# Layer 0's 16 by 16 inverses: masked copies moved to ScalarE on both sides of a transfer, and one load of all diagonal blocks

## The chip, the cores and the metric

The kernel runs on one core of a Trainium2 chip. The metric is device time in microseconds (us) of one execution; times of several runs are given by their median. The engines are TensorE (PE in the profile; its weight loads are PEld), VectorE (DVE), ScalarE (ACT), GpSimd (POOL) and SyncE (SP), which here only issues transfers (DMAs). Each engine works through an instruction queue of its own, whose order is fixed when the kernel is built.

## The reference, cut to what matters

A two-layer trunk over 1024 time steps and 1024 channels. Layer 0 has two groups of heads, each followed chunk by chunk (here 128 steps to a chunk): RWKV-7 (`wkv7_scan`) and gated DeltaNet. In chunked form both need, for each chunk and head, the inverse of a unit triangular 128 by 128 matrix:

```
    amat = jnp.where(strict, jnp.einsum('bhncd,bhnsd->bhncs', kb, k) * decay, 0.0)
    rhs = jnp.concatenate([v * beta[..., None], kb * jnp.exp(gc)[..., None]], -1)
    sol = lax.linalg.triangular_solve(amat, rhs, left_side=True, lower=True, unit_diagonal=True)
```

Then come the output projection, a squared-ReLU MLP and a gated embedding, and in layer 1 chunked attention with the same MLP; all of these are large matrix products.

## The kernel before, in words

Layer 0 works through 16 units: for each half of the time steps (512 each) and each of four head pairs, one RWKV unit and one DeltaNet unit in turn. A unit passes the stages `in` (projections), `front`, `mid`, `back` and `post`; several units are under way at once, as generators that a small planner (`Trunk.run`) takes forward by a virtual clock, with waiting times from the table `LAT`. The planner sets the order in which the code is written down. From that, the scheduler of the tile framework makes the order of each engine's queue at build time, with a cost model of its own: an instruction goes in where the model thinks that its inputs are ready. On the chip that order is kept.

Each unit has one inversion, so there are 16. The odd ones (1, 3, ... 15) are RWKV's with eight 128 by 128 matrices (tile `N`, four chunks of two heads), the even ones DeltaNet's with four (tile `Ng`). `inverse_start`, called in `front`, does the smallest blocks, and its steps are one chain:

- L411: the matrices go to scratch memory (`scr`), a row of 512 bytes for each matrix and partition, all matrices of a partition side by side (4 KB for eight).
- L415: the 16 by 16 diagonal blocks come back as `Bq` (`subb` in the profile), one block to a partition, 8 blocks to a matrix; one load for each matrix, eight or four.
- L423 and L425: GpSimd sets the start of the inverse `X` (tile `sub`), upper triangle and ones on the diagonal, in two passes. L430 and L432: 14 steps of a product and a sum on GpSimd.
- L433 and L434: GpSimd makes two masked copies, one transposed, of the blocks that have an even number.
- L436 and L438: copy, inverse and masked copy go out to scratch memory (`z`), 768 numbers for each block, and come back as `Xp` with 16 rows of a block on 16 partitions, 48 numbers each.

`inverse_end`, called in `mid`, builds the 128 by 128 inverse from them with small matmuls into a PSUM tile `iz`; its first matmuls are `iz<-Xp,N` (or `iz<-Xp,Ng`). ScalarE copies its results (L463, L479, L488, L490, L501).

Beside it, TensorE runs the projections, `dps<-xg,whi` and `dps<-xg,wlo`: 128 by 512 products, 24 to a 128-row weight tile. Each weight tile is loaded by SP (`wraw`), and split by ScalarE (`whi`, L318) and VectorE (`wlo`, L319). In `back`, RWKV's recurrence has for each chunk a copy on ScalarE of `bk` to `bm` (L999), a copy `W<-ch` (L1036) and matmuls that need them (`pm<-AR,bm`, `ch<-W,F`). `tp<-AR,bk` and `sc<-KQ` are the matmuls that give `N` and `Ng`; `o` (L1070, L1072) and `po` belong to the ends of recurrences.

Of the kernel before, what the change touches and what calls it, by code (L numbers as in the profile page):

```python
# [8 lines left out]
F32 = mybir.dt.float32  # L9
F32R = mybir.dt.float32r  # L10
I32 = mybir.dt.int32
AF = mybir.ActivationFunctionType
ALU = mybir.AluOpType
# [4 lines left out]
P = 128  # L18
# [94 lines left out]
class Trunk:  # L113
# [140 lines left out]
    def masks(self, cst):  # L254
# [4 lines left out]
        for j, op in enumerate((ALU.is_ge, ALU.is_gt, ALU.is_ge)):  # L259
# [12 lines left out]
        nc.vector.tensor_reduce(h[:, 2:3], self.ident.rearrange("p (n two) -> p n two", two=2)[:, :, 0],  # L272
                                op=ALU.add, axis=AX.X)
        self.Z16 = cst.tile([P, 8, 32], F32, tag="Z16", name="Z16")
# [132 lines left out]
    def inverse_start(self, B, G):  # L407
        nc, fr = self.nc, self.fr
        NP = 8 * G
        scr = self.dr.tile([P, G, P], F32, tag=f"scr{G}", name="scr", bufs=2)  # L410
        nc.sync.dma_start(out=scr, in_=B)  # L411
        Bq = fr.tile([NP, 16, 16], F32, tag="subb", name="subb")
        for g in range(G):
            b = scr[0:1, 0:1, 0:1]
            nc.sync.dma_start(out=Bq[8 * g:8 * g + 8],  # L415
                              in_=bass.AP(tensor=b.tensor, offset=b.offset + g * P,
                                          ap=[[16 * G * P + 16, 8], [G * P, 16], [1, 16]]))

        XX = fr.tile([NP, 16, 3, 16], F32, tag="sub", name="sub")
        X = XX[:, :, 1, :]  # L420
        tmp = fr.tile([NP, 64], F32, tag="subt", name="subt")
        E = nc.gpsimd
        E.affine_select(out=X, in_=Bq, compare_op=ALU.is_gt, fill=1.0, base=0, pattern=[[-1, 16], [1, 16]],  # L423
                        channel_multiplier=0)
        E.affine_select(out=X, in_=X, compare_op=ALU.is_ge, fill=0.0, base=0, pattern=[[-1, 16], [1, 16]],  # L425
                        channel_multiplier=0)
        for i in range(1, 15):
            n = 15 - i
            o = tmp[:, 0:i * n].rearrange("p (i n) -> p i n", i=i)
            E.tensor_tensor(o, X[:, 0:i, i:i + 1].broadcast_to((NP, i, n)),  # L430
                            Bq[:, i:i + 1, i + 1:16].broadcast_to((NP, i, n)), op=ALU.mult)
            E.tensor_tensor(X[:, 0:i, i + 1:16], X[:, 0:i, i + 1:16], o, op=ALU.add)  # L432
        E.tensor_scalar(XX[:, :, 0, :], X.rearrange("p r c -> p c r"), self.half[0:NP, 2:3], None, op0=ALU.mult)  # L433
        E.tensor_scalar(XX[:, :, 2, :], X, self.half[0:NP, 2:3], None, op0=ALU.mult)  # L434
        z = self.dr.tile([NP, 768], F32, tag=f"z{G}", name="z", bufs=2)
        nc.sync.dma_start(out=z, in_=XX.rearrange("p r w c -> p (r w c)"))  # L436
        Xp = self.mid.tile([P, G, 64], F32, tag="Xp", name="Xp", bufs=2)
        nc.sync.dma_start(out=Xp[:, :, 0:48], in_=z.rearrange("(g b) (r c) -> (b r) g c", g=G, r=16))  # L438
        return Xp

    def inverse_end(self, Xp, B, N, F):

        nc, h2 = self.nc, self.mid
        V, A, G = nc.vector, nc.scalar, nc.gpsimd
        T1, cur, X2 = Xp[:, :, 0:16], Xp[:, :, 16:32], Xp[:, :, 32:64]
        m2 = self.half[:, 1:2]
        quad = [slice(32 * i, 32 * i + 32) for i in range(4)]
        up, lo = slice(0, 64), slice(64, 128)

        def bank(w):  # L450
            return self.psm.tile([P, N, w], F32, tag="iz", name="iz")

        def new(nm, w):
            return h2.tile([P, N, w], F32, tag=nm, name=nm)


        pz = bank(16)
        for g in range(N):
            for q in quad:
                self.mm(pz[q, g, :], B[q, g, q], T1[q, g, :], start=True, stop=True)  # L460
        TZ = self.TZ[:, 0:N]
        T2, Z = TZ[0:96, :, 0:32], TZ[:, :, 0:32]
        A.activation(self.Z16[:, 0:N, 0:16], pz, AF.Copy, scale=m2)  # L463
        yield f"inverse{N}_0"
        px = bank(16)
        for g in range(N):
            for q in quad:
                self.mm(px[q, g, :], self.Z16[q, g, :], cur[q, g, :], start=True, stop=True)
        V.scalar_tensor_tensor(X2[:, :, 16:32], cur, m2, px, op0=ALU.mult, op1=ALU.add)
        V.transpose(T2, X2[0:96])  # L470
        V.transpose(TZ[quad[1], :, 32:64], X2[quad[1]])
        yield f"inverse{N}_1"

        pz = bank(32)
        for g in range(N):
            for i in (0, 2):
                self.mm(pz[quad[i + 1], g, :], B[quad[i], g, quad[i + 1]], T2[quad[i], g, :], start=True, stop=True)
        for i, cp in ((0, A.copy), (2, V.tensor_copy)):
            cp(Z[quad[i + 1]], pz[quad[i + 1]])  # L479
        for i, cp in ((2, V.tensor_copy), (3, A.copy), (0, V.tensor_copy), (1, A.copy)):  # L480
            cp(F[quad[i], :, quad[i]], X2[quad[i]])
        yield f"inverse{N}_2"
        px = bank(32)
        for g in range(N):
            for i in (0, 2):
                self.mm(px[quad[i], g, :], Z[quad[i + 1], g, :], X2[quad[i + 1], g, :], start=True, stop=True)
            self.mm(px[quad[1], g, :], X2[quad[1], g, :], Z[quad[1], g, :], start=True, stop=True)
        A.copy(Z[quad[1]], px[quad[1]])  # L488
        for i, cp in ((2, V.tensor_copy), (0, A.copy)):
            cp(F[quad[i], :, quad[i + 1]], px[quad[i]])  # L490
        yield f"inverse{N}_4"

        part = lambda t, e: t[:, e::2, :]

        def both(ps, f):
            for g in range(N):
                f(ps[up if g % 2 == 0 else lo, g, :], g)

        def out(dst, ps):
            for e, r in ((0, up), (1, lo)):  # L500
                A.copy(part(dst, e), part(ps[r], e))  # L501
        pz = bank(64)
        both(pz, lambda o, g: self.mm(o, B[up, g, lo], TZ[up, g, :], start=True, stop=True))
        out(TZ[lo], pz)
        yield f"inverse{N}_5"
        px = bank(64)
        both(px, lambda o, g: self.mm(o, TZ[lo, g, :], F[lo, g, lo], start=True, stop=True))
        out(F[up, :, lo], px)
        yield f"inverse{N}_6"
# [1754 lines left out]
```

## Time and profile before

| what | value |
|---|---|
| median of 3 runs (lowest to highest) | 2938.03 us (2933.39 to 2940.38) |
| the profiled execution, its span | 2942.2 us, 2940.5 us |
| TensorE busy, of the span | 2866.6 us, 97% |
| VectorE, ScalarE, GpSimd busy | 72%, 50%, 14% |
| mean granted TensorE clock | 0.989 |

Times in the views count from the span's start; the profiled execution is 1.7 us longer than its span. [...] "Idle before" in a row, in square brackets, names what ended an engine's wait.

### The profile page before, as it was taken

The page shows a single profiled execution, that of the slowest core. Times are in us where ns is not written, and L with a number is a line of the kernel's source. Part 1 is how long each engine was busy: PE and PEld are TensorE (multiplying, and loading weights), DVE is VectorE, ACT ScalarE, POOL GpSimd, SP SyncE. Part 2 cuts the span into 40 slices and gives each one's busy share as a digit, 9 for nine tenths or more (in the row PEclk, how much of TensorE's full clock was granted, in tenths as well). Part 3 has the DMA queues.
Part 4 walks back from the last instruction along what each step waited for, and adds up shares of the span by engine and source line. Part 5 has one row for each costly group of instructions (what it writes and reads, how often), then busy time and mean ns, then how long its engine had stood idle before and what let it go on. Part 6 is the DMA issues. An engine that isn't in the chain of part 4 may idle for free.

```text
span 2940.5 us, 46945 instructions
## 1 busy us (share of the span) xinstructions
PE 2866.6 (97%) x17286; PEld 2413.2 (82%) x17286; DVE 2107.7 (72%) x4228; ACT 1466.9 (50%) x2904; POOL 408.8 (14%) x834
## 2 busy tenths in 40 slices
PE   8999999999999999999999999999999999999999
PEld 6777778787778888888888999999888888888877
DVE  6666744555668777788887677776858777878884
ACT  4454532344347555544444566665847555544441
POOL 5434421333120000000000111111300000000000
PEclk9999999999999999999999999999999999999999
DMA  7634434333456444754424211110465444754423
GB/s 266 211 132 157 143 105 146 96 111 110 133 204 204 150 147 155 265 179 151 151 89 143 74 45 57 56 46 28 140 228 201 151 147 154 272 172 150 154 93 116
DMA packets 209479, 421.43 MB, mean 143 GB/s; under 512 B 46832, under 2 KB 49120, under 8 KB 209248
## 3 DMA queue, kind: packets, MB, share of 16 engines
q1 hardware_dynamic: 178432, 362.31, 37.6%
q10 hardware_dynamic: 30816, 56.11, 5.0%
q8 instruction: 136, 2.23, 0.3%
q14 instruction: 95, 0.78, 0.1%
HBM read 287.47 MB, written 130.87 MB: 142 GB/s over the span
## 4 chain that ended last, share of the span: by engine, by line
PE 73%; DVE 11%; DMA 8%; ACT 3%; issue 2%; POOL 2%; SPq 0%; ACTq 0%; DVEq 0%; POOLq 0%
PE dps L180 60%; PE ch L180 2%; PE po L180 2%; PE iz L180 2%; DVE act L1338 1%; PE pt L195 1%; PE pm L180 1%; PE sn L180 1%; PE tp L180 1%; DMA pn<-pnd 1%; POOL subt L430 1%; POOL sub L432 1%; DMA late<-hd 1%; DMA hb<-late 1%; DMA Xp<-z 1%
## 5 line engine op out<-in xcount | busy, mean ns | idle before, releaser
L180 PE MATMUL dps<-r,act 128*128 128x512 f32 x3720 | 865.9, 389 | 4.1 <-DVE r L1338 1.3
L180 PEld LDWEIGHTS dps<-r,act 128*128 128x128 f32 x3720 | 697.1, 188 | 152.7 <-DVE r L1338 2.1
L180 PE MATMUL dps<-xg,whi 128*128 128x512 f32 x1184 | 395.3, 414 | 11.2 <-ACT whi L318 7.5
L180 PE MATMUL dps<-wq,act 128*128 128x384 f32 x1536 | 302.2, 340 | 2.4 <-DVE vs L1994 1.5
L180 PEld LDWEIGHTS dps<-wq,act 128*128 128x128 f32 x1536 | 263.1, 188 | 5.6 <-DVE vs L1994 2.6
L180 PEld LDWEIGHTS dps<-xg,whi 128*128 128x128 f32 x1184 | 218.0, 195 | 56.9 <-ACT whi L318 7.5
L180 PE MATMUL dps<-xg,wlo 128*128 128x512 f32 x592 | 239.2, 405 | 2.0 <-DVE wlo L319 2.0
L1337 ACT CAST act<-act 128x512 fp32r<-128x512 f32 (+2 forms) x281 | 159.0, 599 | 139.9 <-PE dps L180 62.7
L1338 DVE TENSOR_TENSOR act<-act 128x512 fp32r<-128x512 f32 (+2 forms) x281 | 177.8, 661 | 3.5 <-ACT act L1337 3.4
L180 PE MATMUL dps<-act 128*128 128x512 f32 x720 | 173.5, 389 | 0.0
L1337 ACT CAST act<-late 128x512 fp32r<-128x512 f32 x210 | 123.8, 620 | 90.4 <-PE dps L180 61.8
L180 PE MATMUL dps<-late,act 128*128 128x512 f32 x672 | 164.5, 389 | 0.0
L1338 DVE TENSOR_TENSOR act<-late,act 128x512 fp32r<-128x512 f32 x210 | 139.4, 687 | 28.1 <-ACT act L1337 27.9
L180 PEld LDWEIGHTS dps<-act 128*128 128x128 f32 x720 | 135.2, 188 | 28.1
L180 PEld LDWEIGHTS dps<-late,act 128*128 128x128 f32 x672 | 125.9, 188 | 26.0
L180 PE MATMUL dps<-xw,act 128*128 128x512 f32 x576 | 143.8, 389 | 0.4 <-ACT act L1337 0.4
L1605 DVE TENSOR_TENSOR xw<-xw,dps 128x512 f32<-128x512 f32 x192 | 130.0, 682 | 16.4 <-PE dps L180 15.9
L180 PEld LDWEIGHTS dps<-xg,wlo 128*128 128x128 f32 x592 | 114.5, 193 | 27.7 <-DVE wlo L319 3.1
L180 PEld LDWEIGHTS dps<-xw,act 128*128 128x128 f32 x576 | 108.0, 188 | 23.2 <-ACT act L1337 0.8
L2117 ACT ACTIVATE pb<-pb,mx 128x640 f32<-128x640 f32 (+4 forms) x128 | 89.2, 697 | 51.9 <-DVE mx L2111 50.8
L1863 POOL MEMSET far<- 128x256 f32 x1 | 0.3, 312 | 756.0 <-PE dps L180 756.0
L1337 ACT CAST r<-act 128x512 fp32r<-128x512 f32 x126 | 76.3, 618 | 56.3 <-PE dps L180 37.8
(522 smaller groups left out, 5377.7 us busy)
## 6 DMA issues: line engine op xcount, KB each, us to landing
hb<-late ACTq DMA_DIRECT2D x196, 256.0 KB
act<-hb SPq DMA_DIRECT2D x158, 256.0 KB
late<-in_w SPq DMA_DIRECT2D x60, 512.0 KB
act<-in_w SPq DMA_DIRECT2D x112, 256.0 KB
braw<-hb SPq DMA_DIRECT2D x80, 256.0 KB
wd<-whi SPq DMA_DIRECT2D x32, 512.0 KB
wd<-wlo SPq DMA_DIRECT2D x32, 512.0 KB
wlo<-wd SPq DMA_DIRECT2D x32, 512.0 KB
```

The costliest lines, as they stand in the source:

```text
L180: return self.begin(self.nc.tensor.matmul(out, lhsT, rhs, start=start, stop=stop, skip_group_check=again))
L195: return self.begin(self.nc.tensor.transpose(out, in_, ident))
L430: E.tensor_tensor(o, X[:, 0:i, i:i + 1].broadcast_to((NP, i, n)), Bq[:, i:i + 1, i + 1:16].broadcast_to((NP, i, n)), op=ALU.mult)
L432: E.tensor_tensor(X[:, 0:i, i + 1:16], X[:, 0:i, i + 1:16], o, op=ALU.add)
L1337: A.copy(hi, s)
L1338: V.tensor_tensor(lo, s, hi.bitcast(F32), op=ALU.subtract)
L1605: V.tensor_tensor(x[n][:, hs[hf]], x[n][:, hs[hf]], ps, op=ALU.add)
L1863: nc.gpsimd.memset(self.far, 0.0)
L2117: A.activation(S, S, AF.Exp, bias=mx[:, 1:2] if nf else mx[:, 0:1], scale=-1.0, accum_out=l)
```

## The change

The matrices go out in two transfers, one for each half of them, into scratch memory laid out with a distance of P\*P+P numbers from matrix to matrix, so that all 16 by 16 blocks lie at one constant distance and come back by one load. The start of the inverse is one masking pass and a write of ones on the diagonal. GpSimd's two masked copies are gone: the transposed one is made by ScalarE before the outward transfer (new L434), and the other by ScalarE from the returned tile (new L447, at the head of `inverse_end`), so `z` has 512 numbers for each block instead of 768, and `Xp` gets 32 in a row instead of 48. From L447 on, line numbers after the change are one higher.

```diff
     def inverse_start(self, B, G):
...
-        scr = self.dr.tile([P, G, P], F32, tag=f"scr{G}", name="scr", bufs=2)
-        nc.sync.dma_start(out=scr, in_=B)
+        pitch = P * P + P
+        scr = self.dr.tile([G, pitch], F32, tag=f"scr{G}", name="scr", bufs=2)
+        d = scr[0:1, 0:1]
+        for g in (G // 2, 0):
+            nc.sync.dma_start(out=bass.AP(tensor=d.tensor, offset=d.offset + g * pitch,
+                                          ap=[[P, P], [pitch, G // 2], [1, P]]), in_=B[:, g:g + G // 2])
         Bq = fr.tile([NP, 16, 16], F32, tag="subb", name="subb")
-        for g in range(G):
-            b = scr[0:1, 0:1, 0:1]
-            nc.sync.dma_start(out=Bq[8 * g:8 * g + 8],
-                              in_=bass.AP(tensor=b.tensor, offset=b.offset + g * P,
-                                          ap=[[16 * G * P + 16, 8], [G * P, 16], [1, 16]]))
-
-        XX = fr.tile([NP, 16, 3, 16], F32, tag="sub", name="sub")
+        nc.sync.dma_start(out=Bq, in_=bass.AP(tensor=d.tensor, offset=d.offset,
+                                              ap=[[16 * P + 16, NP], [P, 16], [1, 16]]))
+
+        XX = fr.tile([NP, 16, 2, 16], F32, tag="sub", name="sub")
...
-        E.affine_select(out=X, in_=Bq, compare_op=ALU.is_gt, fill=1.0, base=0, pattern=[[-1, 16], [1, 16]],
+        E.affine_select(out=X, in_=Bq, compare_op=ALU.is_gt, fill=0.0, base=0, pattern=[[-1, 16], [1, 16]],
                         channel_multiplier=0)
-        E.affine_select(out=X, in_=X, compare_op=ALU.is_ge, fill=0.0, base=0, pattern=[[-1, 16], [1, 16]],
-                        channel_multiplier=0)
+        E.memset(flat[:, 16:512:33], 1.0)
...
-        E.tensor_scalar(XX[:, :, 0, :], X.rearrange("p r c -> p c r"), self.half[0:NP, 2:3], None, op0=ALU.mult)
-        E.tensor_scalar(XX[:, :, 2, :], X, self.half[0:NP, 2:3], None, op0=ALU.mult)
-        z = self.dr.tile([NP, 768], F32, tag=f"z{G}", name="z", bufs=2)
-        nc.sync.dma_start(out=z, in_=XX.rearrange("p r w c -> p (r w c)"))
+        nc.scalar.activation(XX[:, :, 0, :], X.rearrange("p r c -> p c r"), AF.Copy, scale=self.half[0:NP, 2:3])
+        z = self.dr.tile([NP, 512], F32, tag=f"z{G}", name="z", bufs=2)
+        nc.sync.dma_start(out=z, in_=flat)
         Xp = self.mid.tile([P, G, 64], F32, tag="Xp", name="Xp", bufs=2)
-        nc.sync.dma_start(out=Xp[:, :, 0:48], in_=z.rearrange("(g b) (r c) -> (b r) g c", g=G, r=16))
+        nc.sync.dma_start(out=Xp[:, :, 0:32], in_=z.rearrange("(g b) (r c) -> (b r) g c", g=G, r=16))
         return Xp
...
     def inverse_end(self, Xp, B, N, F):
...
         m2 = self.half[:, 1:2]
+        A.activation(X2[:, :, 0:16], cur, AF.Copy, scale=self.half[:, 0:1])
         quad = [slice(32 * i, 32 * i + 32) for i in range(4)]
```

The planner's table and rules are untouched, but the scheduler, which sees other instructions, makes another order of the queues. On TensorE the orders agree up to shortly before the first `iz` matmul of the fourth inversion, and again from the end of layer 0 on, but for some 26 rows in layer 1. Three places follow. Numbers behind names tell tiles apart and differ between the two builds.

ScalarE's queue at the third inversion, inside the recurrence of an RWKV unit, before the change:

```order
L479 COPY TZ_239<-iz_2078 32x4x32
L1168 ACTIVATE f_2187<-KQ_1794 128x512
L1128 ACTIVATE f_2293<-raw_1475,vecs_60 128x512
L999 COPY bm_241<-bk_1372 64x256
L1036 COPY W_1954<-ch_1950 128x128
L488 COPY TZ_239<-iz_2101 32x4x32
```

The same place after it:

```order
L480 COPY TZ_239<-iz_2057 32x4x32
L1169 ACTIVATE f_2166<-KQ_1772 128x512
L1129 ACTIVATE f_2267<-raw_1462,vecs_60 128x512
L434 ACTIVATE sub_1703<-sub_1703,half_145 64x16x16
L1000 COPY bm_241<-bk_1358 64x256
L1037 COPY W_1932<-ch_1928 128x128
L489 COPY TZ_239<-iz_2080 32x4x32
```

The new masked copy of this inversion's blocks (L434) stands ahead of the copies `bm` and `W` of another unit's recurrence; nothing else moved here.

ScalarE's queue at the fourth inversion, after the change (`bh` is a cast in the front of the next RWKV unit, `whi` are weight tiles for projections):

```order
L1222 ACTIVATE U_2376<-ch_2374,cs_1146 128x128
L880 ACTIVATE f_2792<-raw_2128,d_omu_69 128x512
L1000 COPY bm_241<-bk_2392 64x256
L434 ACTIVATE sub_2227<-sub_2227,half_145 32x16x16
L967 CAST bh_2795<-f_2790 128x512
L318 CAST whi_2615<-wraw_2613 128x1024
L318 CAST whi_2707<-wraw_2705 128x1024
L447 ACTIVATE Xp_2262<-Xp_2262,half_145 128x4x16
```

Before the change the rows are the same without L434 and L447; now the first of them stands ahead of the casts of two weight tiles, and the second behind them.

TensorE's queue just ahead of the ninth inversion's first `iz` matmul, before the change:

```order
L180 MATMUL dps_5388<-xg_4099,whi_5382 128x512 x2
L180 MATMUL dps_5388<-xg_4099,wlo_5383 128x512
L180 MATMUL dps_5388<-xg_4104,whi_5382 128x512 x2
L180 MATMUL dps_5388<-xg_4104,wlo_5383 128x512
L180 MATMUL ch_5418<-U_5408,b_4259 128x128
L180 MATMUL po_5335<-b_4313,U_5408 128x128
L180 MATMUL iz_5685<-Xp_5119,N_4990 32x16 x25
```

The same after it:

```order
L180 MATMUL dps_5196<-xg_4063,whi_4805 128x512 x2
L180 MATMUL ch_5279<-Sg3_196,KQ_4003 128x128
L180 MATMUL dps_5196<-xg_4063,wlo_4806 128x512
L195 MATMUL pm_6023<-ident_62,bk_4892 128x128 x4
L180 MATMUL pp_5289<-hsel_151,o_5253 128x2 x4
L180 MATMUL po_5278<-b_4381,Sg3_196 128x128
L180 MATMUL iz_5629<-Xp_5062,N_4941 32x16 x6
```

The first `iz` matmul stood a whole weight tile later, behind two steps of a DeltaNet recurrence; now it follows that recurrence's first `po`. Between the last `tp<-AR,bk` (which completes `N`) and the first `iz` matmul there were 47 `dps` matmuls and are now 29. For the other RWKV inversions from the fifth on the counts are 53 and 48 (fifth), 39 and 32 (seventh), 117 and 102, 66 and 78, 69 and 33 (fifteenth).

## Rows read from the trace of the kernel before

**Rows 1.** Busy time by windows (length, five engines), granted clock, DMA share, GB/s.
```profile
80.00:810.00 730.00, 702.61 (x6585) 564.17 (x6584) 448.28 (x1130) 301.44 (x738) 247.65 (x614) 0.97 0.40 134
810.00:2940.00 2130.00, 2097.78 (x10420) 1799.18 (x10418) 1603.25 (x2991) 1127.31 (x2102) 118.48 (x113) 1.00 0.43 142
```

**Rows 2.** Waits in 80 to 810 us: us in total, times, longest.
```profile
PE iz L180 <- DMA Xp<-z: 13.9, 6, 5.6
```

**Rows 3.** Timeline of TensorE: start, length, instruction, idle before it.
```profile
123.45 0.29 PE L180 MATMUL iz<-Xp,N 32*32 32x16 f32 x2 [5.60 <-DMA Xp<-z]
...
193.29 0.20 PE L180 MATMUL iz<-Xp,N 32*32 32x16 f32 x2 [0.72 <-DMA Xp<-z]
...
535.21 0.62 PE L180 MATMUL iz<-Xp,Ng 32*32 32x16 f32 x32 [2.72 <-DMA Xp<-z]
```

**Rows 4.** Windows as in rows 1, three stretches of lowered clock.
```profile
121.89:132.13 10.24, 8.68 (x32) 6.47 (x36) 1.39 (x2) 1.04 (x1) 1.15 (x3) 0.50 0.82 302
360.82:364.23 3.41, 3.41 (x15) 2.44 (x14) 2.29 (x16) 0.37 (x1) 0.00 (x0) 0.50 0.20 77
534.90:541.73 6.83, 6.52 (x59) 4.93 (x60) 1.36 (x4) 0.72 (x2) 3.33 (x11) 0.50 0.55 162
```

**Rows 5.** Timeline of SP's issues, third inversion.
```profile
165.87 2.85 SPq L415 DMA_DIRECT2D subb<-scr  x8
...
187.82 0.46 SPq L436 DMA_DIRECT2D z<-sub  x1
190.42 0.37 SPq L438 DMA_DIRECT2D Xp<-z  x1
```

**Rows 6.** Timeline of GpSimd, third inversion.
```profile
170.14 0.97 POOL L423 TENSOR_SCALAR_AFFINE_SELECT sub<-subb 64x256 f32<-64x256 f32 x1 [2.64 <-DMA subb<-scr]
171.18 0.98 POOL L425 TENSOR_SCALAR_AFFINE_SELECT sub<-sub 64x256 f32<-64x256 f32 x1
...
185.74 1.16 POOL L433 TENSOR_SCALAR sub<-sub,half 64x256 f32<-64x256 f32 x1
```

**Rows 7.** Timeline of SP's issues, fourth inversion.
```profile
210.64 1.38 SPq L415 DMA_DIRECT2D subb<-scr  x4
```

**Rows 8.** Timeline of GpSimd, fourth and ninth inversion.
```profile
213.51 0.50 POOL L423 TENSOR_SCALAR_AFFINE_SELECT sub<-subb 32x256 f32<-32x256 f32 x1 [11.34 <-DMA subb<-scr]
...
230.38 1.18 POOL L433 TENSOR_SCALAR sub<-sub,half 32x256 f32<-32x256 f32 x1
...
445.79 1.14 POOL L433 TENSOR_SCALAR sub<-sub,half 64x256 f32<-64x256 f32 x1
```

**Rows 9.** ScalarE, groups by shape, 90 to 800 us: busy us, mean ns.
```profile
L481 ACT COPY F<-Xp 32x256 f32<-32x256 f32 x16 | 6.4, 403 | 4.4 <-DVE Xp L469 4.2
...
L463 ACT ACTIVATE Z<-iz,half 128x128 f32<-128x128 f32 x8 | 3.0, 376 | 15.9 <-PE iz L180 15.9
```

**Rows 10.** Timeline of ScalarE, third and fourth inversion.
```profile
176.57 0.71 ACT L1128 ACTIVATE f<-raw,vecs 128x512 f32<-128x512 f32 x1
177.31 0.40 ACT L999 COPY bm<-bk 64x256 f32<-64x256 f32 x1
177.73 0.27 ACT L1036 COPY W<-ch 128x128 f32<-128x128 f32 x1
...
224.02 0.62 ACT L966 CAST bh<-f 128x512 fp32r<-128x512 f32 x1 [0.99 <-DVE f L963]
224.55 2.00 ACT L318 CAST whi<-wraw 128x1024 fp32r<-128x1024 f32 x2
```

**Rows 11.** Timeline of TensorE, third and ninth inversion.
```profile
178.05 0.66 PE L180 MATMUL ch<-W,F 128*128 128x64 f32 x4
...
443.74 0.47 PE L180 MATMUL po<-b,Sg 128*128 128x128 f32 x2
...
454.37 0.61 PE L180 MATMUL iz<-Xp,N 32*32 32x16 f32 x50
```

**Rows 12.** The chain of work that ended last: start, us, what.
```profile
309.90 5.45 PE dps L180 x23
```

More of the change, by code (lines that the diff above doesn't have):

```diff
@@ L409, in inverse_start @@
         NP = 8 * G
-        scr = self.dr.tile([P, G, P], F32, tag=f"scr{G}", name="scr", bufs=2)
-        nc.sync.dma_start(out=scr, in_=B)
-        Bq = fr.tile([NP, 16, 16], F32, tag="subb", name="subb")
-        for g in range(G):
-            b = scr[0:1, 0:1, 0:1]
-            nc.sync.dma_start(out=Bq[8 * g:8 * g + 8],
-                              in_=bass.AP(tensor=b.tensor, offset=b.offset + g * P,
-                                          ap=[[16 * G * P + 16, 8], [G * P, 16], [1, 16]]))
-        XX = fr.tile([NP, 16, 3, 16], F32, tag="sub", name="sub")
+        pitch = P * P + P
[4 more added lines that the diff above has]
+                                          ap=[[P, P], [pitch, G // 2], [1, P]]), in_=B[:, g:g + G // 2])
+        Bq = fr.tile([NP, 16, 16], F32, tag="subb", name="subb")
+        nc.sync.dma_start(out=Bq, in_=bass.AP(tensor=d.tensor, offset=d.offset,
+                                              ap=[[16 * P + 16, NP], [P, 16], [1, 16]]))
+        XX = fr.tile([NP, 16, 2, 16], F32, tag="sub", name="sub")
         X = XX[:, :, 1, :]
+        flat = XX.rearrange("p r w c -> p (r w c)")
         tmp = fr.tile([NP, 64], F32, tag="subt", name="subt")
         E = nc.gpsimd
-        E.affine_select(out=X, in_=Bq, compare_op=ALU.is_gt, fill=1.0, base=0, pattern=[[-1, 16], [1, 16]],
+        E.affine_select(out=X, in_=Bq, compare_op=ALU.is_gt, fill=0.0, base=0, pattern=[[-1, 16], [1, 16]],
                         channel_multiplier=0)
-        E.affine_select(out=X, in_=X, compare_op=ALU.is_ge, fill=0.0, base=0, pattern=[[-1, 16], [1, 16]],
-                        channel_multiplier=0)
+        E.memset(flat[:, 16:512:33], 1.0)
         for i in range(1, 15):
```

## The prediction

> **What bounds the kernel now.** I read busy time by windows first. From 80 to 810 us, where the 16 inversions lie, TensorE is busy for 702.6 of 730 us; after that for 2097.8 of 2130 [rows 1]. So TensorE sets the end, and what this change can give or take is TensorE's idle time in the first stage, 27.4 us, and time lost to a lowered clock. The list of waits then says how much of it is the inversion's: six waits for the returned tile `Xp`, 13.9 us together, the longest 5.60 [rows 2, 3]. [...] The other ten inversions return in time: their chain is hidden behind projections.
>
> **The chain, step by step.** In the third inversion the eight loads start at 165.87 and GpSimd's first pass at 170.14, 4.27 us later; with four loads that is 213.51 - 210.64 = 2.87 [rows 5 to 8]. One load of all blocks moves 1024 pieces of 64 bytes. The nearest row is the return of `Xp`, 1024 pieces of 192 bytes: 190.42 to 193.29, 2.87 us [rows 3, 5]. Bounds are no gain and the whole of the seven issues saved, 7 x 2.85/8 = 2.5 us; I take 2.87, a gain of 1.4 with eight matrices, and 0.3 with four. The second outward issue costs at most one issue, 0.36 us, and the first half can leave before the last matrices are done, so I take 0 of a range of ±0.4. The second masking pass (0.98 us with its slot of 1.04 here, about 0.5 where its twin L423 took 0.50 [rows 6, 8]) makes way for 16 ones per partition, 0.1 us by estimate, bounded by nothing and that pass: gain 0.9 here, 0.5 elsewhere. The two masked copies end with the chain: 187.82 - 185.74 = 2.08 us on GpSimd [rows 5, 6], against one copy on ScalarE of 0.40 (256 elements a partition, 403 ns [rows 9]) and 0.1 to hand over; gain 1.6. The outward copy carries two thirds of the bytes; it took 2.60 us with its issue [rows 5] and I take off 0.3, bounded by 0 and 0.9. So `Xp` returns some 3.8 us earlier with eight matrices and 2.7 with four. ScalarE has 32 more short copies, some 12 us, on an engine that is idle for 430 of these 730 us [rows 1]: as work they cost nothing. The copy after the return lies beside the first `iz` matmuls.
>
> If only this counted, the 5.60 us wait would shrink to about 1.8 and the others vanish.
>
> **What the new order makes of it.** ScalarE begins its instructions in the order of its queue: at the third inversion a scaled copy, `bm`, `W`, one behind the other [rows 10]. The first masked copy now waits on ScalarE for the end of GpSimd's 28 products and sums, and holds all that stands behind it. [...]
>
> Third inversion: `bm` ran at 177.31, `W` from 177.73 to 178.00, and TensorE took `W` at 178.05 [rows 10, 11]. TensorE's order up to there is unchanged. GpSimd's sums ended where L433 began, 185.74 [rows 6]; earlier by 1.4 and 0.9 that is 183.4. Masked copy 0.40, `bm` 0.40, `W` 0.27: 184.5. TensorE waits **6.4 us** where it had no wait.
>
> Fourth inversion: the sums ended at 230.38 [rows 8], now 0.3 and 0.5 earlier, 229.6. Behind the masked copy (0.3) stand the cast of `bh` (0.6) and the first weight cast (2.00/2): 231.5; in the old trace that cast was done at 225.6 [rows 10]. Counting the matmuls from `sc<-KQ` at 5.45/23 = 0.24 us for each 512 columns [rows 12], and 0.02 to 0.46 for the smaller forms, TensorE comes to this weight tile at about 226.7. Wait **4.8 us**.
>
> Ninth inversion: here TensorE itself comes too early. The first `iz` matmul now follows the `po` that began at 443.74; it stood at 454.37, just as `Xp` came back [rows 11]. With `Xp` 3.8 us earlier, at 450.6, and TensorE at the place at 444.0, the wait is **6.6 us**, where there was next to none.
>
> For the others I did the same: the end of the sums or the return of `Xp`, moved earlier by the amounts above, against the place of what stands behind it, counted along the new order. The results are estimates: first inversion 4.5 (5.60 before: the hold delays the evictions that free its PSUM bank), second 1, fifth 3, sixth 0.6, seventh 7, eighth 1.5, tenth 1, eleventh 1, twelfth 1.6, thirteenth and fourteenth none, fifteenth 8 (36 `dps` fewer stand ahead of its `iz`: 8.6 us less cover, and ScalarE is held as well), sixteenth 4. That is 33. The waits of the whole stage would be 6.4 + 4.8 + 6.6 + 33 = 51 us, against 13.9: +37. Some of the other 13.5 us that TensorE idles in the stage now falls into the new waits; I take 5 off: +32.
>
> The clock: 10.2 us were lost for 13.9 waited, 0.74 for 1. On 32 us that would be 24; but the chain goes on while TensorE is slow, so a second wait of the same inversion shrinks. Bounds 0 and 24, and I take 10, as most new waits come two to an inversion. Sum: +42 on the profiled execution's 2942.2, thus 2984; that execution is 4.2 us above the median of its runs, so **2980 us**.
>
> **The rivals.**
> *Faster.* ScalarE's holds hurt no one, and TensorE finds `Xp` in time: 13.9 - 1.8 = 12 us of waiting and most of the 10.2 us of clock are gained, some 22 us: 2916. For it speaks that four of the 16 places show next to no wait in my count. Against it: third and ninth inversion, where row and order leave little room. It would win if the sums ended 6 us earlier than I have them.
> *No change.* The holds are taken up by weights already split, and eat the gain: 2932 to 2944.
> *Half the loss.* While TensorE and ScalarE wait, VectorE dries up too, and GpSimd runs undisturbed: the same pass took 0.97 us at 170.14 and 0.50 at 213.51 [rows 6, 8]. If each of some ten held chains is 1.5 us shorter, 15 us of waiting and 5 of clock are not lost: 2960. [...]
> *Worse.* In the fourth and fifth inversion SP's queue has `z` and `Xp` directly behind the load, so that weight transfers queue behind a chain of 15 us. If weights run short besides, at some four places for 5 us, and the clock takes the full 24: 2942.2 + 32 + 24 + 20 - 4.2 = 3014.
>
> That the change does nothing is excluded by the build: GpSimd has 32 instructions fewer and ScalarE 32 more.
>
> **How the numbers follow.** Likeliest, the sum: 0.47, 2980, with a range of its own from 2966 to 2998. Half the loss 0.22; worse 0.15; no change 0.07; faster 0.09. Below 2940 lie the faster case and half of no change, 0.13; above 3012 about half of worse, 0.07. So 2940 to 3012 holds 8 in 10. About 0.2%, 6 us, is what a measurement of this kernel tells from no change: faster 0.09, same 0.07, slower 0.84.
>
> **What would show it.** GpSimd's chain should be shorter by 2 to 3 us, and loads to first pass by 1.4 with eight matrices. The list of waits should have ScalarE's masked copy waiting for GpSimd's last sum in most of the 16, 3 to 12 us each, and at the third inversion `ch<-W` idle for some 6 us. Waits of `iz` for `Xp` should grow at the seventh, ninth, fifteenth and sixteenth and go at the third, fifth and tenth. The clock should be at 0.50 behind these. I am wrong if ScalarE waits for GpSimd for less than about 2 us each time, or if TensorE's busy share of the stage rises; and in the size, if the clock's losses differ, which I have only as a ratio.

## The result, and the profile after

| what | after |
|---|---|
| median of 4 runs (lowest to highest) | 2978.48 us (2971.88 to 2983.00) |
| the profiled execution, its span | 2979.7 us, 2977.9 us |
| ratio to the kernel before (median of 4 runs: 2936.43) | 1.0143, 95% interval 1.0129 to 1.0157 |
| TensorE busy, of the span | 2888.2 us, 97% |
| VectorE, ScalarE, GpSimd busy | 71%, 50%, 12% |
| mean granted TensorE clock | 0.981 |

The change costs 42 us, 1.4%. To see where, one needs a place that both executions pass with the same work done: the first `dps<-r,act`, the start of layer 0's MLP. It is at 904.69 us before and at 943.67 after, so the whole difference of the spans (37.4 us) lies ahead of it. Busy time by windows up to there, columns as in [rows 1], first of the kernel before:

```profile
80.00:904.70 824.70, 791.34 (x7005) 636.52 (x7004) 517.74 (x1252) 352.23 (x825) 268.56 (x628) 0.97 0.43 142
```

and of the kernel after:

```profile
80.00:943.70 863.70, 812.11 (x7000) 650.77 (x6999) 516.75 (x1251) 367.12 (x852) 209.00 (x596) 0.94 0.41 134
```

Some 7000 matmul records (7005 and 7000) take TensorE 20.8 us longer, at a mean clock of 0.94 in place of 0.97, and it idles 863.7 - 812.1 = 51.6 us in place of 33.4. So about half of the loss, 18.2 us, is waiting, and half is clock. The largest piece of the second is one stretch that begins in the seventh inversion's wait, where [rows 4] had 3.41 us at half clock (windows view of after):

```profile
359.10:386.40 27.30, 26.39 (x251) 20.78 (x251) 17.04 (x71) 10.37 (x26) 0.64 (x2) 0.50 0.09 21
```

What TensorE waits for has changed altogether. The list of waits of the kernel after up to the same place, for TensorE:

```profile
PE ch L180 <- ACT W L1037: 13.4, 5, 5.3
PE ch L180 <- DVE W L1217: 5.3, 3, 4.3
...
PE pm L180 <- ACT bm L1000: 3.9, 1, 3.9
...
PE iz L180 <- DMA Xp<-z: 3.0, 3, 1.2
PE dps L180 <- DVE raw L709: 2.7, 1, 2.7
```

and for ScalarE:

```profile
ACT sub L434 <- POOL sub L433: 62.0, 14, 8.9
...
ACT Xp L447 <- DMA Xp<-z: 28.7, 14, 5.1
```

The waits for `Xp` [rows 2] have shrunk from 13.9 to 3.0 us. In their place stand `W`, `bm` and evictions (copies of results out of PSUM), and ScalarE's new copies wait for GpSimd and for the transfer in 14 of 16 inversions each.

The third inversion shows both sides. The chain, as SP's issues (timeline of after, answering to [rows 5]):

```profile
157.17 0.62 SPq L417 DMA_DIRECT2D subb<-scr  x1
175.28 0.47 SPq L436 DMA_DIRECT2D z<-sub  x1
177.60 0.37 SPq L438 DMA_DIRECT2D Xp<-z  x1
```

on GpSimd (answering to [rows 6]):

```profile
160.07 0.50 POOL L425 TENSOR_SCALAR_AFFINE_SELECT sub<-subb 64x256 f32<-64x256 f32 x1 [18.07 <-DMA subb<-scr]
160.63 0.12 POOL L427 MEMSET sub<- 64x16 f32 x1
```

on ScalarE (answering to [rows 10]):

```profile
169.35 0.71 ACT L1129 ACTIVATE f<-raw,vecs 128x512 f32<-128x512 f32 x1
174.53 0.72 ACT L434 ACTIVATE sub<-sub,half 64x256 f32<-64x256 f32 x1 [4.47 <-POOL sub L433]
175.28 0.40 ACT L1000 COPY bm<-bk 64x256 f32<-64x256 f32 x1
175.70 0.27 ACT L1037 COPY W<-ch 128x128 f32<-128x128 f32 x1
```

and on TensorE (answering to [rows 11]):

```profile
176.02 1.12 PE L180 MATMUL ch<-W,F 128*128 128x64 f32 x4 [5.28 <-ACT W L1037]
```

From the load's issue to that of `Xp` the chain takes 20.4 us, 4.1 less than before (24.55). By the same timelines of SP, over all 16 inversions it is 5.9 us shorter on average with eight matrices (24.6 to 18.7) and 4.0 with four (21.4 to 17.4). But `bm` and `W` of another unit stand behind the masked copy, and TensorE stands still for them. In the fourth inversion the hold goes one engine further (timelines of after; ScalarE, VectorE, TensorE):

```profile
225.05 0.72 ACT L434 ACTIVATE sub<-sub,half 32x256 f32<-32x256 f32 x1 [3.26 <-POOL sub L433]
225.68 0.60 ACT L967 CAST bh<-f 128x512 fp32r<-128x512 f32 x1
...
226.31 0.69 DVE L968 TENSOR_TENSOR bh<-f,bh 128x512 fp32r<-128x512 f32 x1 [2.92 <-ACT bh L967]
226.92 1.28 DVE L709 TENSOR_TENSOR raw<-dps,rsbc 128x512 f32<-128x512 f32 x2
...
227.75 0.70 PE L180 MATMUL dps<-xg,whi 128*128 128x512 f32 x2 [2.70 <-DVE raw L709]
```

The cast `bh` is late, so VectorE waits with its difference `bl` (L968), and the eviction behind that (L709), which TensorE needs, is late too.

### The profile page after: what moved, and what is told of

It is laid out like the page before. It is cut to its first block, busy times and chain, and to the rows that moved or that the text cites. A ratio compares the mean times of both kernels' runs of the same rounds, so it can differ in the third digit from the quotient of the medians.

```text
span 2977.9 us, 46835 instructions
## 1 busy us (share of the span) xinstructions
PE 2888.2 (97%) x17286; PEld 2427.7 (82%) x17286; DVE 2108.6 (71%) x4228; ACT 1483.8 (50%) x2936; POOL 349.7 (12%) x802
## 4 chain that ended last, share of the span: by engine, by line
PE 67%; DVE 13%; DMA 9%; ACT 4%; POOL 3%; issue 3%; SPq 0%; ACTq 0%; DVEq 0%; POOLq 0%
PE dps L180 55%; PE po L180 2%; DVE act L1339 2%; PE ch L180 2%; DMA late<-in_w 2%; POOL subt L431 2%; POOL sub L433 1%; PE pt L195 1%; PE iz L180 1%; PE sn L180 1%; PE pm L180 1%; DMA hb<-late 1%; DMA pn<-pnd 1%; DVE late L1487 1%; DMA late<-hd 1%
## 5 line engine op out<-in xcount | busy, mean ns | idle before, releaser
L180 PE MATMUL dps<-xg,whi 128*128 128x512 f32 x1184 | 401.7, 418 | 15.2 <-ACT whi L318 8.2
L2118 ACT ACTIVATE pb<-pb,mx 128x640 f32<-128x640 f32 (+4 forms) x128 | 89.1, 697 | 51.6 <-DVE mx L2112 50.6
L180 PE MATMUL po<-ptile,vs 128*128 128x256 f32 (+1 forms) x576 | 98.5, 282 | 4.6 <-ACT ptile L364 2.1
```

The costliest lines, as they stand in the source:

```text
L180: return self.begin(self.nc.tensor.matmul(out, lhsT, rhs, start=start, stop=stop, skip_group_check=again))
L2118: A.activation(S, S, AF.Exp, bias=mx[:, 1:2] if nf else mx[:, 0:1], scale=-1.0, accum_out=l)
```

## The experiments

Two theories could explain a slower kernel. **H**: ScalarE's queue is held by copies that wait for GpSimd. **O**: the new order of the queues itself is bad, TensorE's above all. Twelve runs, each against the kernel before on the same chip, whose median there was 2935.1 to 2937.2 us; ratios with 95% intervals.

**The hold alone.** Before, with one small copy on ScalarE behind GpSimd's last sum:

```diff
+        nc.scalar.copy(tmp[:, 32:48], X[:, 0, :])
```

> The kernel before, with one more instruction in each of the 16 inversions: behind GpSimd's last sum, ScalarE copies 16 numbers of each partition of the inverse into the scratch tile `tmp`. Nobody needs the result; loads, passes, masked copies and transfers are as before, and on TensorE 6 of 14794 rows change place. Theory H (what costs is that ScalarE's queue is held while an instruction in it waits for GpSimd): ScalarE waits for GpSimd in most of the 16, TensorE waits for what stands behind, and the time is 2955 to 2985 us, against 2936 before. Theory O (what costs is the new order of the queues, TensorE's above all): the order is the old one, so 2934 to 2942 us.

Measured: 2940.4 us, ratio 1.0012 (1.0000 to 1.0025): 3 us, inside O's range. ScalarE was held as foreseen, yet TensorE hardly lost (lists of waits of this run, ScalarE and TensorE):

```profile
ACT subt L433 <- POOL sub L432: 45.7, 16, 9.0
...
PE iz L180 <- DMA Xp<-z: 4.9, 4, 2.9
PE iz L180 <- ACT TZ L502: 4.2, 2, 3.4
PE dps L180 <- ACT whi L318: 3.8, 2, 3.1
```

The holds made new waits of some 10 us, and the waits for `Xp` behind them fell from 13.9 to 4.9, since the chain goes on while TensorE stands. H alone, as it was forecast here, falls.

**Parts of the change, each in the order that the scheduler then makes.** Masked copies back on GpSimd:

```diff
-        nc.scalar.activation(XX[:, :, 0, :], X.rearrange("p r c -> p c r"), AF.Copy, scale=self.half[0:NP, 2:3])
...
+        E.tensor_scalar(XX[:, :, 0, :], X.rearrange("p r c -> p c r"), self.half[0:NP, 2:3], None, op0=ALU.mult)
+        E.tensor_scalar(XX[:, :, 2, :], X, self.half[0:NP, 2:3], None, op0=ALU.mult)
...
-        A.activation(X2[:, :, 0:16], cur, AF.Copy, scale=self.half[:, 0:1])
```

> The kernel after, with both masked copies back on GpSimd ahead of the transfer (768 numbers for each block, no copy on ScalarE); the two outward transfers, the one load and the single masking pass stay. TensorE's order differs from that of before in 2106 rows of 14794 (the kernel after: 2470). Theory H: no hold on ScalarE, the chain is shorter by 2.3 us with eight matrices and 0.8 with four, so 2915 to 2938 us. Theory O: most of the new order is still there, so 2960 to 2980 us. Theory L (one load and a larger distance in scratch memory cost something themselves): loads to GpSimd's first pass take longer than the 4.27 us of before, and 2940 to 2960 us.

Measured: 2960.4 us, ratio 1.0077 (1.0053 to 1.0100). No masked copy holds ScalarE, and it is still slower, as O has it (the time lies where the ranges of O and L meet; L falls below, in the run of the same work in the old order): waits for `Xp` of 16.3 us in 6.

The same exchange the other way round, in the kernel before:

> The kernel before, with the two masked copies made by ScalarE as in the change (one ahead of the transfer, one from the returned tile, 512 numbers for each block), but with the old eight or four loads and both masking passes. TensorE's order differs from that of before in 941 rows of 14794. Theory H: the holds of the kernel after are all here and, as GpSimd ends 0.8 to 2.3 us later, a little longer: 2970 to 2995 us. Theory O: less than half of the new order, so 2940 to 2960 us.

Measured: 2954.0 us, ratio 1.0058 (1.0038 to 1.0077), as O has it, although ScalarE waits for GpSimd 47.7 us in 14 places.

The first copy on GpSimd, the second on ScalarE:

```diff
-        nc.scalar.activation(XX[:, :, 0, :], X.rearrange("p r c -> p c r"), AF.Copy, scale=self.half[0:NP, 2:3])
+        E.tensor_scalar(XX[:, :, 0, :], X.rearrange("p r c -> p c r"), self.half[0:NP, 2:3], None, op0=ALU.mult)
```

> The kernel after, with the transposed masked copy ahead of the transfer made by GpSimd (as it was), the second one by ScalarE from the returned tile. GpSimd has one masked copy fewer than before. Theory H, first copy alone: no wait of ScalarE for GpSimd, the chain is shorter by some 3 us than before and the time is 2912 to 2936 us. Rival S (the second copy's waits for the returned tile, 28.7 us in 14 waits in the kernel after, hold ScalarE's queue as the first one's do): 2945 to 2965 us. Theory O: 2960 to 2980 us.

Measured: 2968.8 us, ratio 1.0103 (1.0077 to 1.0129), inside O's range and above that of S. The hold has moved to the second copy (list of waits of this run, ScalarE, then TensorE):

```profile
ACT Xp L447 <- DMA Xp<-z: 79.3, 15, 14.7
...
PE ch L180 <- ACT W L1037: 18.2, 4, 8.2
```

Each of these three has an order of its own (2106 and 941 rows of TensorE moved in the first two), so order and work could not be told apart in them. For the next runs they were: edges between neighbours of a written-out queue, which fix the order and make no engine wait.

```diff
+def in_order(tc, nc, own):
...
+    edge = mybir.DependencyInfo(mybir.DependencyClass.NoSync, mybir.DependencyReason.DATA)
...
+        for u, v in zip(queue, queue[1:]):
+            tc.add_manual_dep(rows[v], rows[u].name, edge, reason="order")
```

**The change in the old order.**

> The kernel after, with the queues of all engines forced into the order that they have in the kernel before, by ordering edges that make no engine wait. Only the change's own instructions (masked copies on ScalarE, masking pass and ones on GpSimd, transfers to and from scratch memory) stand where the scheduler puts them between the others. TensorE's and VectorE's order is that of before in every row. Theory O (the new order of the queues is what costs, the change itself gains): 2905 to 2932 us. Theory H (holds of ScalarE's queue cost, in any order): 2955 to 2980 us.

Measured: 2939.9 us, ratio 1.0013 (1.0004 to 1.0022). Some 39 us of the 43 are gone, so H's range is missed, but the gain that O expected is missing too.

**The old work in the new order.**

> The opposite: the work of the kernel before (eight or four loads, two passes, two masked copies on GpSimd, nothing new on ScalarE) with the queues forced into the order of the kernel after. TensorE's and VectorE's order is that of after in every row. Theory O: as slow as after or slower, since the chain is 3 us longer in the same places: 2970 to 2995 us. Theory H: no hold, so 2930 to 2945 us.

Measured: 3000.3 us, ratio 1.0221 (1.0205 to 1.0236), 5 us above O's range. Here the order shows bare: the waits for `Xp` are 40.0 us in 8, where the same work in its own order has 13.9 in 6 (list of waits of this run, then timeline of TensorE, inversions 5, 7, 9 and 15):

```profile
PE iz L180 <- DMA Xp<-z: 40.0, 8, 11.7
...
286.98 0.26 PE L180 MATMUL iz<-Xp,N 32*32 32x16 f32 x2 [4.36 <-DMA Xp<-z]
376.13 0.36 PE L180 MATMUL iz<-Xp,N 32*32 32x16 f32 x10 [6.62 <-DMA Xp<-z]
484.52 0.40 PE L180 MATMUL iz<-Xp,N 32*32 32x16 f32 x12 [8.29 <-DMA Xp<-z]
784.42 1.03 PE L180 MATMUL iz<-Xp,N 32*32 32x16 f32 x58 [11.70 <-DMA Xp<-z]
```

**The new order without the first hold.**

```diff
-        nc.scalar.activation(XX[:, :, 0, :], X.rearrange("p r c -> p c r"), AF.Copy, scale=self.half[0:NP, 2:3])
+        nc.scalar.activation(XX[:, :, 0, :], Bq.rearrange("p r c -> p c r"), AF.Copy, scale=self.half[0:NP, 2:3])
```

> The kernel after with its own order of all queues (forced, the same in every row), but ScalarE's first masked copy reads the diagonal blocks as they were loaded, and not their inverses (so the inverses' transposed copies are left out of the computation). It waits for the load and GpSimd's first pass alone, which are over some 14 us earlier. Theory H: the holds (62 us of ScalarE's time in 14 waits) are gone and with them most of the loss, 2935 to 2955 us. Theory O: 2970 to 2985 us, as the kernel after.

Measured: 2969.2 us, ratio 1.0113 (1.0095 to 1.0132), 9 us below the kernel after. That is no clean removal: the second copy now holds the queue, 77.5 us in 16 waits where it was 28.7 (list of waits of this run):

```profile
ACT Xp L447 <- DMA Xp<-z: 77.5, 16, 13.2
```

**Masks on GpSimd in the old order.** The run of that name, its queues in the order of before.

> The kernel of the run masks_on_gpsimd (one load, one masking pass, both masked copies on GpSimd, 2960 us in its own order) with the queues of all engines forced into the order of the kernel before. Theory O: the chain is shorter by 2.3 us with eight matrices and nothing else changes, so 2915 to 2932 us. Rival L (the new load costs something itself): 2945 us and more.

Measured: 2922.4 us, ratio 0.9959 (0.9944 to 0.9975). The one load, the single pass and the two outward transfers gain 13 us together, and L falls; 2960 us in their own order was the order's doing.

**Without both holds, in either order.** First copy on GpSimd; the second stands on ScalarE behind a copy for which ScalarE waits in any case:

```diff
-        A.activation(X2[:, :, 0:16], cur, AF.Copy, scale=self.half[:, 0:1])
...
-        A.activation(self.Z16[:, 0:N, 0:16], pz, AF.Copy, scale=m2)
+        z = A.activation(self.Z16[:, 0:N, 0:16], pz, AF.Copy, scale=m2)
+        ins = A.activation(X2[:, :, 0:16], cur, AF.Copy, scale=self.half[:, 0:1]).ins
```

> The kernel after without its two holds: the transposed masked copy ahead of the transfer is GpSimd's, as before, and ScalarE's copy from the returned tile stands directly behind the copy of the first `iz` results (`Z16`), for which ScalarE waits anyway. All queues are forced into the order of the kernel before. Theory B (order and holds both cost, the work gains): the chain is 1 us shorter than that of the run masks_gpsimd_old_order, so 2910 to 2922 us. Theory O (order alone): as the change in the old order, 2932 to 2943 us.

Measured: 2918.3 us, ratio 0.9945 (0.9928 to 0.9961): as B has it, and faster than both kernels.

> The same work as in the run no_holds_old_order, with all queues forced into the order of the kernel after. Theory B: the chain is some 0.5 us longer than after's, but no instruction holds ScalarE's queue; the order's cost stays and the holds' goes: 2945 to 2966 us. Theory O: nothing gained beside the kernel after, 2970 to 2985 us.

Measured: 2963.9 us, ratio 1.0099 (1.0085 to 1.0113), as B has it. The holds gone, `Xp` is waited for again, 21.8 us in 5 (list of waits of this run, then timeline of TensorE, inversions 5, 7, 9 and 15):

```profile
PE iz L180 <- DMA Xp<-z: 21.8, 5, 8.9
...
272.26 0.25 PE L180 MATMUL iz<-Xp,N 32*32 32x16 f32 x2 [4.62 <-DMA Xp<-z]
359.13 0.36 PE L180 MATMUL iz<-Xp,N 32*32 32x16 f32 x10 [5.59 <-DMA Xp<-z]
461.46 0.40 PE L180 MATMUL iz<-Xp,N 32*32 32x16 f32 x12 [1.84 <-DMA Xp<-z]
752.38 1.03 PE L180 MATMUL iz<-Xp,N 32*32 32x16 f32 x58 [8.89 <-DMA Xp<-z]
```

**TensorE's queue alone in the old order.**

> The kernel after with all its own work and its holds; only TensorE's queue is forced into the order of the kernel before, and the scheduler places all else round it. If it is TensorE's order that costs (it comes to the first `iz` and to the recurrences at other places), the time is that of the change in the old order, 2935 to 2945 us. If it is the order of the transfers or of ScalarE and VectorE, 2955 to 2980 us.

Measured: 2961.6 us, ratio 1.0091 (1.0078 to 1.0105), inside the second forecast. Yet 17 of the 39 us that all queues together give back come back here. With TensorE's order given, the scheduler puts the first copy ahead of other things, and the waits that are left stand behind it: of TensorE's seven longest ahead of the MLP, six (24.0 us together) end within 3.4 us of the start of a masked copy. One of them (timelines of this run; ScalarE, VectorE, TensorE):

```profile
548.53 0.72 ACT L434 ACTIVATE sub<-sub,half 32x256 f32<-32x256 f32 x1 [5.09 <-POOL sub L433]
549.15 0.60 ACT L967 CAST bh<-f 128x512 fp32r<-128x512 f32 x1
...
549.79 0.69 DVE L968 TENSOR_TENSOR bh<-f,bh 128x512 fp32r<-128x512 f32 x1 [4.48 <-ACT bh L967]
550.40 0.28 DVE L1063 SCALAR_TENSOR_TENSOR S<-S,ee,ch 128x64 f32<-128x64 f32 x1
...
550.73 1.11 PE L180 MATMUL ch<-b,PMQ 128*128 128x64 f32 x4 [2.89 <-DVE S L1063]
```

**Another order with nothing else.**

```diff
-    "end_front": 46.33,
+    "end_front": 46.43,
```

> The kernel before with one number changed: the planner's waiting time `end_front` is 46.43 instead of 46.33. No instruction is added or taken away; TensorE's order differs from that of before in 1209 of 14794 rows, all behind row 4178, in the second half of layer 0. If nearly any other order than the one in the kernel before is worse (it was found by trying), the time is 2945 to 2970 us. If the order of the kernel after is bad for a reason of its own (the scheduler takes the inversion's chain for shorter than it is on the chip, and brings its consumers too early), 2930 to 2942 us.

Measured: 2936.1 us, ratio 1.0006 (0.9996 to 1.0016), inside the second forecast. In this one case 1209 moved rows cost nothing: a new order is not bad only because it is new. The orders that the scheduler made for other work (after, and the three runs of parts) took 2954 to 2978 us.

The six kernels that settle it, medians in us (from several chips), with TensorE's busy and idle time from 80 us to the start of the MLP in their profiles:

| work | order of before | order of after |
|---|---|---|
| that of before | 2935.4; busy 791.3, idle 33.4 | 3000.3; busy 811.6, idle 73.9 |
| the change, with its holds | 2939.9; busy 791.9, idle 31.0 | 2978.5; busy 812.1, idle 51.6 |
| the change without holds | 2918.3; busy 784.1, idle 20.5 | 2963.9; busy 797.1, idle 49.8 |

Go from before to the change without holds, then to the change with its holds, both in the left column, and then to the right: the work gains 17, the holds cost 22, the order 39; together +43. O alone falls as well, since taking the holds away gains 22 and 15 us in one and the same order. The three do not simply add: the holds cost 15 in the new order, and the order costs 46 without holds and 65 with the old work. What is called the holds here includes that the first copy goes back to GpSimd. The hold alone cost only 3 us in the kernel before. There it took the place of waits for `Xp`; in the change without holds in the old order only 2.0 us of these are left that a hold could replace, and the change has a second hold besides. Which of the two makes the difference was not separated.

## Why the prediction came out, step by step

**What bounds the kernel.** Right: the whole loss is in the stage of the inversions, as TensorE's idle time and clock.

**The chain.** Right for the third inversion: 4.1 us shorter. The prediction says 3.8, but its own terms (1.4, 0.9, 1.6 and 0.3) add up to 4.2. From the load's issue to GpSimd's first pass 2.90 (2.87 predicted); the outward copy 2.32 in place of 2.60 (0.3 off, as predicted); ones 0.12. The masked copy was mis-sized: 0.72 us on ScalarE, not 0.40. Over all 16 the sum was too small: 5.9 and 4.0 us shorter on average, not 3.8 and 2.7. Of this, 1.8 and 1.0 us lie between GpSimd's first product and last sum, for which the sum had nothing. That a shorter chain is worth some 20 us if nothing else happens is shown too: the work without holds (not quite the change, as its first copy is GpSimd's) takes 2918 us in the old order, with 2.0 us of waits for `Xp`, where the faster rival had 2916 and 1.8. That rival failed on the other two steps, not on this one.

**The holds.** The mechanism was right and is seen row by row: third inversion 5.28 us (6.4 predicted), fourth 2.70 (4.8, and not by way of the weight cast that I named but by `bh` and VectorE), fifth 3.15 (3), seventh 4.52 (7), tenth 3.88 (1), fifteenth 4.32 (8; again by way of VectorE). At the seventh and fifteenth I had expected waits of `iz` for `Xp`. ScalarE waits for GpSimd for 3 us or more in 12 of the 16 (timeline of TensorE of after, inversions 5, 7, 10 and 15):

```profile
273.08 0.66 PE L180 MATMUL ch<-W,F 128*128 128x64 f32 x4 [3.15 <-ACT W L1037]
359.87 1.11 PE L180 MATMUL ch<-W,F 128*128 128x64 f32 x4 [4.52 <-ACT W L1037]
558.43 1.22 PE L180 MATMUL pm<-AR,bm 128*128 128x128 f32 x3 [3.88 <-ACT bm L1000]
757.94 0.77 PE L180 MATMUL ch<-W,F 128*128 128x128 f32 x2 [4.32 <-DVE W L1217]
```

In the rows of the third inversion above, ScalarE kept to the order of its queue: the masked copy ran from 174.53 to 175.25, `bm` began at 175.28 and `W` at 175.70. The first inversion's 4.5 did not come.

**TensorE too early.** The mechanism was right, its place in the sum wrong. With the old chain the new order gives a wait of 8.29 us at the ninth inversion, and at the fifteenth, where 36 `dps` fewer stand ahead of the `iz`, 11.70. In the kernel after, the fifth, seventh and fifteenth have a hold first. TensorE is late by it, and `Xp` is there when TensorE arrives, or nearly so (1.19 us at the fifteenth); without holds the new order has waits of 4.62, 5.59 and 8.89 there. So hold and early `iz`, which I took for two waits of an inversion, are there one lateness that shows at whichever comes first, and the wait of `iz` at the seventh is gone where I expected it to grow. The ninth is another case. There I had 6.6 us; in the kernel after it is 1.17, and 1.84 without holds, so no hold hides it (timelines of SP and TensorE, before and then after):

```profile
428.37 3.22 SPq L415 DMA_DIRECT2D subb<-scr  x8
...
452.10 0.61 SPq L417 DMA_DIRECT2D subb<-scr  x1
...
471.11 0.30 PE L180 MATMUL iz<-Xp,N 32*32 32x16 f32 x12 [1.17 <-DMA Xp<-z]
```

Counted from the load's issue, TensorE had `Xp` after 19.0 us, where I had worked out 22.2, and came to the place after 17.8, where I had 15.6. So +32 us of idle time was too much: 18.2 were measured.

**The clock.** Too little: +10 predicted, 20.8 more busy time measured for the same matmuls, near my upper bound of 24. The ratio of 0.74 rests on three stretches, 20.48 us at a granted clock of 0.50 [rows 4], of which it takes half, 10.2 us, as lost. No run shows that half. Four `sc<-KQ` in a row took 2.08 us at 0.50 (361.12) and 1.11 at 1.00 (192.89, both in the trace after), by which I estimate some 9.6 us lost in the three. A clock of 0.97 over 730 us [rows 1] means by estimate some 22 us lost in the stage. My reason for taking less (a second wait of the same inversion shrinks) was an argument about waits and was put into the clock, where it did not hold. The two errors, 14 too much and 11 too little, offset each other, so that 2980 comes so near to 2978.5 is luck; the direction and the two causes are not.

**Weights of the two causes.** The prediction speaks of holds first. The runs turn that round: with the change's work the order costs 39 to 46 us (65 with the old work), the holds 15 to 22.

**The rivals.** "Half the loss" had GpSimd quicker while VectorE is held. That GpSimd is quicker is shown, and near the supposed size: the 448 products and sums take 151.0 us after and 163.3 before, 0.8 us for each inversion, and from the first to the last of them an inversion takes 1.4 us less on average, where 1.5 in ten of them was supposed. Yet the loss came in full. That VectorE's idleness is the reason is not shown: the first pass (L423, 64 by 256) took 0.97 us at 170.14 and 0.50 at 252.76 of the trace before, with VectorE at work both times, and no run here separates its idleness from other reasons. "Worse" was wrong in its weights: no long wait for a weight transfer on account of SP's queue is in the list (TensorE waits 0.9 us for `whi` and 0.5 for `wlo`, ScalarE 0.8 for `wraw`).

**What stays open.** Why the scheduler's order is too early can only be argued: it would have placed the consumers by an idea of the chain's length that shrank by more than the chain did (36 `dps`, 8.6 us, at the fifteenth inversion, where the chain is 6.5 us shorter after, 24.2 to 17.7). How the order's cost divides among the queues was not separated: with TensorE's queue alone forced, the scheduler made another order of the rest. No kernel was forced into its own order with its work unchanged either; that the edges cost nothing is argued from the two kernels with edges that are faster than any without (2918 and 2922 us).

## What to carry to other kernels

Where a scheduler orders the queues, an edit is two edits, the work and the order; compare the orders before looking for a cause in the work, and hold the order fixed by edges without waits to see each alone. An instruction that waits long does not belong in the queue of an engine that others need (here the holds cost 15 to 22 us): it should stand behind something for which that engine waits anyway, as the second copy behind `Z16`, or on the engine that makes its input. Waits of one chain are not to be summed: take one away and the next shows, as ScalarE's wait for `Xp` grew from 28.7 to 77.5 us when the first hold was gone.

## What the hardware showed that was not expected

ScalarE's transposing masked copy of 256 numbers in each of 64 partitions took 0.72 to 0.77 us, where a plain copy of as many took 0.40 [rows 9]; in 32 partitions it took 0.72 to 0.78. The new copy has a scale as well, and how much the transposing costs was not separated: 128 numbers took 0.38 with a scale (L463 in [rows 9]) and 0.27 without (`W` in [rows 10]). And TensorE stayed at a granted clock of 0.50 for 27.3 us while it was busy for 26.39 of them, from 0.8 us before the end of a wait of 4.52 us on; only 9 of the 251 matmul records in it are 128 by 512 `dps<-xg`. The run without holds in the new order, with a wait of 5.59 us for `Xp` there, has 20.5 us at half clock at the same place (355.3 to 375.8).
